# Linear memory's projection as seven block products in a one-core encoder layer

## The chip, the cores and the metric

The kernel runs on one core of one Trainium2 chip. The metric is the device time of one execution in microseconds (us), as the median of several executions. Of one execution there is also a trace from the hardware profiler: every instruction on each engine with its start and length. The engines are called as in the profile: PE is TensorE's matmul and PEld its weight load, DVE is VectorE, ACT is ScalarE, POOL is GpSimd, SP is SyncE, which here only issues DMAs.

## The reference

One inference step of one encoder layer, on 576 tokens (512 of a new stream, called the prompt, and 64 that continue a running stream) of width D = 1024, all in float32:

```
h = LN1(alpha*x + 0.5*FFN1(x))
z = h @ w_in      # q, k, v, o, i, f of the linear memory | q, k, v of attention | gates g_m, g_a
m = mLSTM(h)      # 4 heads of 256: head outputs normalised, times a gain and sigmoid(o)
y_ml  = m @ w_ml_proj                       # 1024 x 1024: the product that is changed
y_att = att @ w_att_proj
merged = sigmoid(g_m) * y_ml + sigmoid(g_a) * y_att
h = LN2(alpha*h + merged @ w_out)
y = LN3(alpha*h + 0.5*FFN2(h))
```

The outputs are y for both streams and the new states of convolution, linear memory and attention.

## The kernel before

Activations lie transposed: eight tiles of 128 features by 576 tokens. Each float32 product is made of three matmuls of rounded parts. A tile is split into **hi** (ScalarE rounds it) and **lo** (the remainder, by VectorE: tile minus hi), for weights and activations, and `mm3` adds hi·hi, hi·lo and lo·hi in PSUM. So every operand costs ScalarE and VectorE one pass each before TensorE can use it, and a weight tile of 128 x 1024 as much as an activation tile.

**Weights.** `plan` (from L430) lists all weight tiles in the order of use. `pump` (L248) loads the next raw tile on SP's queue into one of two `wr` buffers, and splits it into one of four pairs `wh`, `wl`; `take` and `done` (to L317) count them in and out. For the keys of the set ADDED the remainder is made by a transfer instead (`add_lo`, L195): ScalarE writes -hi, and a DMA on GpSimd's queue adds the raw weight from HBM to it.

**Order of the work.** TensorE's program is written in the order in which the Python code emits it; `later(dt, f)` on the object `od` puts f into a heap by due time, counted in TensorE's work, so that short pieces (transposes, norms) stand between the long products. On the other engines a scheduler orders the instructions by priority (`high_priority`, `issue_after`), and each engine works its list strictly in order.

**Stages.** FFN1 and LN1 (`Norm`, L536; `ffn`, L1158), the products with w_in with attention between them, attention's projection (`ap_pair`, L1808), the linear memory's four heads (L1841 to L2143), its projection (L2144 to L2193, 1041.7 to 1092.4 us), the output projection with LN2 (L2196 to L2205), FFN2 and LN3.

**Seven block products.** `seven` (L838) serves the FFNs and attention's projection. A pair of output column tiles j, j+1 (columns 1 and 2) by the two halves of the tokens is a 2 x 2 block product over two halves of the input tiles. In Winograd's form it needs seven products instead of eight, of sums of the weight blocks (`split_ds`, L209: a is the first column's weight as it is, u two sums, t two more, b half the second's) and of sums of the activation blocks (b11, b21, b22 as they are; t1 to t4 sums). Each product is four input tiles by three matmuls, on 288 columns, into one of three PSUM tiles X, Y, Z, in the order a·b11, a·b21, t·t2, u·t1, u·t3, t·b22, b·t4. After product n `step(n)` takes out what is complete.

**The projection.** Head 3 ends with the transposes of its normalised output `hf` and the last gate's product (`gate(7)`, 48 matmuls). `ht_split` splits the eight tiles of m (`HF`, called og in the profile) into hi and lo (`H`). Then eight plain products, one per column tile j, each 48 matmuls: for both halves of the tokens (256 and 320 columns) eight input tiles by three matmuls. `mp_cb` multiplies the result by the gate `sg` (called s in the profile) on VectorE, adds attention's half `matt` on GpSimd, which SP has loaded from HBM (`MD`) for all eight tiles, and splits the sum into `mg`, the output projection's input.

**The residual of LN2.** LN1's output stays in SBUF as hi and lo (it is the input of all products with w_in). LN2 makes alpha·h from it by two VectorE instructions per tile and half (`residual`, L562). LN2's own output is also written to HBM (`XD`, L1156), from where LN3 fetches it as one tile and needs one instruction.

## Time and profile before

| | |
|---|---|
| Executions before | 1549.29, 1549.52, 1552.53 us; median 1549.52 |
| Span of the profiled execution | 1546.8 us (its own time is not listed apart; median less span is 2.7) |
| PE busy | 1531.3 us, 11587 matmuls |
| DVE, ACT, POOL busy | 1160.4, 882.5, 196.6 us |
| Projection | 1041.7 to 1092.4 us, 384 matmuls |

The page gives first the span and the busy time of each engine, then the span in 40 slices with the granted TensorE clock, the DMA queues, the chain of work that ended last, and the costliest groups of instructions. A line of a group or of the timeline names the source line, the engine, the operation, what it writes and reads by the program's names (`wl<-wr,wh`: a weight's remainder from raw and hi), the shape, and in square brackets how long the engine had been idle before it and what ended that. Matmuls are pipelined, so two may overlap in a line of the timeline; the spacing of their starts is their price.

### The profile page before, as it was taken

What the parts mean: (1) busy time and instruction counts of PE and PEld (TensorE: products, weight loads), DVE (VectorE), ACT (ScalarE), POOL (GpSimd) and SP (SyncE); (2) the same over time, 40 slices, a digit from 0 to 9 for tenths busy, and PEclk for the clock granted to TensorE, in tenths of its full rate; (3) what the DMA queues carried; (4) which work ended last, traced back from release to release, by engine and by line L of the source; (5) the groups of instructions that cost most, each with busy time, mean ns of one, the idle gap of its engine ahead of it and who ended that gap; (6) DMA issues with size and microseconds to landing.
All of it is one profiled execution on the core that took longest, in us unless ns stands there. A gap on an engine that the chain in (4) does not pass through costs nothing.

```text
span 1546.8 us, 29458 instructions
## 1 busy us (share of the span) xinstructions
PE 1531.3 (99%) x11587; PEld 1516.3 (98%) x11587; DVE 1160.4 (75%) x2186; ACT 882.5 (57%) x1670; POOL 196.6 (13%) x370
## 2 busy tenths in 40 slices
PE   9999999999999999999999999999999999999997
PEld 9999999999999999999999999999999999999997
DVE  7877778756899767887677577775688787787756
ACT  7545446533766557777864877753456454557323
POOL 1000000100200015545200321102120000001000
PEclk9999999999999999999999999999999999999999
DMA  8322223535544449687544965542653223217244
GB/s 246 109 101 91 93 99 102 130 108 146 172 152 143 156 167 239 153 209 169 139 107 147 283 148 133 130 132 82 199 126 104 108 82 110 82 69 190 78 128 150
DMA packets 82228, 213.18 MB, mean 138 GB/s; under 512 B 9513, under 2 KB 23209, under 8 KB 82089
## 3 DMA queue, kind: packets, MB, share of 16 engines
q1 hardware_dynamic: 66088, 172.29, 33.8%
q0 software_dynamic: 14848, 37.30, 13.7%
q8 instruction: 91, 1.49, 0.4%
q10 hardware_dynamic: 1152, 1.70, 0.3%
q14 instruction: 49, 0.39, 0.1%
HBM read 174.82 MB, written 22.22 MB: 127 GB/s over the span
## 4 chain that ended last, share of the span: by engine, by line
PE 84%; DVE 7%; ACT 3%; DMA 3%; issue 2%; POOL 1%; SPq 0%; ACTq 0%; DVEq 0%; POOLq 0%
PE mm L133 69%; PE aux L133 14%; PE aux L143 2%; DVE wl L150 1%; DVE sc L1537 1%; DVE s L150 1%; DVE s L153 1%; ACT wh L147 1%; ACT sc L147 1%; DMA s<-in_xT 1%; DVE o L150 1%; DVE kl L150 1%; DVE sc L157 1%; DMA wr<-in_w_ap 0%; DMA kh<-kh 0%
## 5 line engine op out<-in xcount | busy, mean ns | idle before, releaser
L133 PE MATMUL mm<-s,wh 128*128 128x288 f32 (+2 forms) x3430 | 700.8, 298 | 0.7 <-DVE s L150 0.2
L133 PEld LDWEIGHTS mm<-s,wh 128*128 128x128 f32 x3430 | 548.3, 189 | 3.8 <-DVE s L150 1.6
L133 PE MATMUL mm<-s,wl 128*128 128x288 f32 (+2 forms) x1705 | 503.3, 295 | 0.0
L133 PEld LDWEIGHTS mm<-s,wl 128*128 128x128 f32 x1705 | 321.1, 188 | 0.2 <-DVE wl L150 0.2
L147 ACT ACTIVATE wh<-wr 128x1024 fp32r<-128x1024 f32 (+2 forms) x136 | 133.0, 979 | 141.0 <-PE mm L133 81.7
L133 PE MATMUL mm<-tx,wh 128*128 128x288 f32 x778 | 158.4, 296 | 0.0
L150 DVE TENSOR_TENSOR wl<-wr,wh 128x1024 fp32r<-128x1024 f32 (+2 forms) x97 | 108.9, 1126 | 57.1 <-ACT wh L147 57.0
L133 PEld LDWEIGHTS mm<-tx,wh 128*128 128x128 f32 x778 | 124.9, 188 | 0.0
L133 PE MATMUL mm<-tx,wl 128*128 128x288 f32 x383 | 113.0, 295 | 0.6 <-DVE wl L150 0.6
L925 ACT ACTIVATE wh<-wt 128x1024 fp32r<-128x1024 f32 x53 | 56.2, 1060 | 88.4 <-DVE wt L150 88.4
L150 DVE TENSOR_TENSOR wl<-wt,wh 128x1024 fp32r<-128x1024 f32 x53 | 64.7, 1222 | 52.3 <-ACT wh L925 51.0
L133 PE MATMUL mm<-h,wh 128*128 128x256 f32 (+2 forms) x384 | 78.3, 295 | 0.0
L150 DVE TENSOR_TENSOR wl<-wu,wh 128x1024 fp32r<-128x1024 f32 x50 | 61.2, 1224 | 21.6 <-ACT wh L925 21.6
L197 POOL DMA_DIRECT2D s<-s x16 | 13.7, 854 | 495.0 <-ACT s L147 252.8
L133 PEld LDWEIGHTS mm<-tx,wl 128*128 128x128 f32 x383 | 72.0, 188 | 0.9 <-DVE wl L150 0.9
L147 ACT ACTIVATE h<-h 128x288 f32<-128x288 f32 x80 | 34.9, 437 | 65.2 <-DVE h L150 65.1
L925 ACT ACTIVATE wh<-wu 128x1024 fp32r<-128x1024 f32 x50 | 52.9, 1058 | 32.7 <-PE mm L133 32.5
L150 DVE TENSOR_TENSOR wl<-ws,wh 128x1024 fp32r<-128x1024 f32 x53 | 64.6, 1219 | 0.1
L150 DVE TENSOR_TENSOR ws<-wu 128x1024 f32<-128x1024 f32 x53 | 64.5, 1217 | 0.0
L133 PEld LDWEIGHTS mm<-h,wh 128*128 128x128 f32 x384 | 61.5, 188 | 0.2
L925 ACT ACTIVATE ah<-wu 128x512 fp32r<-128x512 f32 x53 | 33.4, 631 | 44.8 <-PE mm L133 41.3
L133 PE MATMUL mm<-h,wl 128*128 128x256 f32 (+2 forms) x192 | 56.5, 294 | 0.0
(399 smaller groups left out, 3612.6 us busy)
## 6 DMA issues: line engine op xcount, KB each, us to landing
wu<-in_w_gu SPq DMA_DIRECT2D x80, 512.0 KB, 4.3
wr<-in_w_in SPq DMA_DIRECT2D x46, 512.0 KB, 3.7
wr<-in_w_dn SPq DMA_DIRECT2D x40, 512.0 KB, 3.6
wl<-in_w_in POOLq DMA_DIRECT2D x38, 512.0 KB, 6.8
wu<-in_w_in SPq DMA_DIRECT2D x26, 512.0 KB, 4.5
wr<-in_w_dn SPq DMA_DIRECT2D x20, 384.0 KB, 3.7
s<-s POOLq DMA_DIRECT2D x16, 288.0 KB, 3.7
wr<-in_w_ap SPq DMA_DIRECT2D x8, 512.0 KB, 3.6
```

Source lines behind the costliest of these rows:

```text
L133: PE.matmul(out, lhsT, rhs, start=start, stop=stop, **kw)
L143: PE.transpose(out, in_, idn)
L147: return ACT.activation(out, in_, func, **kw)
L150: return (eng or DVE).tensor_tensor(out, a, b, op=op)
L153: return DVE.scalar_tensor_tensor(out=out, in0=a, scalar=s, in1=b, op0=op0, op1=op1)
L157: return (eng or DVE).tensor_scalar(out=out, in0=a, scalar1=s1, scalar2=s2, op0=op0, **kw)
L197: return POOL.dma_start(lo, src, accum_op=ALU.add)
L925: self.last = ACT.activation(hi, src, AF.Copy)
L1537: DVE.tensor_tensor_reduce(out=out, in0=ps, in1=g, op0=ALU.add, op1=ALU.min, scale=-1.0, scalar=3e38, accum_out=acc)
```

## The change

The linear memory's projection takes the form of attention's projection: the plan lists four weights a, u, t, b per pair of column tiles, and `mp_pair` calls `seven`. The rows of w_ml_proj are regrouped on the host, even tiles first, so that the two halves of the input tiles are the first and the second tile of each head. `blocks(i)` makes head i's activation factors: it rounds and subtracts the plain tiles, and makes the four sums of half tiles on VectorE, in place in the two tiles of m; then it splits the sums. The remainder of the sums of heads 0 and 1, and of one of head 2's two, is made by `add_lo`, the rest on VectorE. Heads 0 and 1 are emitted while head 3 is still at work (`first_blocks`), heads 2 and 3 behind it. The remainders of a and b weights are made by `add_lo` too; u and t have their sums and remainders on VectorE, with buffers of their own (`q`). Attention's half is no longer loaded: for three pairs a DMA on GpSimd's queue adds it from HBM into the gated tile, and for the last pair it is loaded into two tiles and added on VectorE.

LN1 now writes its normed output to HBM (`XH`, 16 DMAs on SP's queue), and LN2 fetches it from there (8 DMAs on SP's queue) and needs one residual instruction per tile and half. The arguments `down` and `store` of `Norm` carry what `away` alone said before. Some buffers of the heads move to pools that end earlier (`mq`) to make the room.

In the instruction lists the matmuls of the projection are 336 instead of 384; TensorE's order ahead of the projection is the same.

The diff, cut to its core:

```diff
         def put(a, t):
             n = t.shape[1]
             ds["hi"] = act(hi[:, a:a + n], t)
+            if plan[c][0][0] == "dsmp" and what in "ab":
+                add_lo(lo[:, :n], hi[:, :n], plan[c][1])
+                return
             tt(lo[:, a:a + n], t, f(hi[:, a:a + n]), ALU.subtract)
 
         if what == "a":
             put(0, r1)
         elif what == "u":
-            own = plan[c][0][0] == "dsap" and plan[c][0][1] > 0
-            room = lambda: (slot(F32, opool[0], "o") if own else slot(F32))[:, :512]
+            mp_ = plan[c][0][0] == "dsmp"
+            own = mp_ or plan[c][0][0] == "dsap" and plan[c][0][1] > 0
+            def room():
+                if mp_:
+                    return qpool[0].tile([P, 512], F32, tag="q", name=nm("q"), bufs=4)
+                return (slot(F32, opool[0], "o") if own else slot(F32))[:, :512]
+
             q = ds["q"] = [room() for _ in range(2)]
             ds["r"] = [room() for _ in range(2)] if own else [q[1]] * 2
             r2 = ds["u"]
             for i in range(2):
-                tt(q[i], (r1[:, 512:], r2[:, :512])[i], r2[:, 512:], ALU.add)
+                with tc.issue_after(wst["blocks"].ins) if plan[c][0][:2] == ("dsmp", 2) else nullcontext():
+                    tt(q[i], (r1[:, 512:], r2[:, :512])[i], r2[:, 512:], ALU.add)
             for i in range(2):
                 put(512 * i, q[i])
         elif what == "t":
...
-    plan += [(("mp", j), ins["w_mp"][j]) for j in range(KT)]
+    for j in range(0, KT, 2):
+        a, b = ins["w_mp"][j], ins["w_mp"][j + 1]
+        plan += [(("dsmp", j, x), w) for x, w in (("a", a), ("u", b), ("t", None), ("b", b[:, :512]))]
     plan += [(("o", j), ins["w_o"][j]) for j in range(KT)]
     plan_ffn(2)
...
     class Norm:
-        def __init__(self, xs, scale, eps, gi, final=None, keep=False, away=None):
-            self.away = away
+        def __init__(self, xs, scale, eps, gi, final=None, keep=False, away=None, down=False, store=None):
+            self.away, self.down, self.store = away, down, store
...
                     act(dh, dh, AF.Identity, bias=b_)
-                    if self.away is None:
-                        SP.dma_start(XD[j][:, t0:t0 + n], dh)
+                    SP.dma_start(self.store[j][:, t0:t0 + n], dh)
                     act(hs(hi, hf), dh)
                     tt(hs(lo, hf), dh, hs(f(hi), hf), ALU.subtract)
...
 
-        own = name == "dsap"
+        own = name in ("dsap", "dsmp")
         product(X, "a", 1, "b11", True, False)
...
 
-    XD = [away("xd") for _ in range(KT)]
+    XD, XH = [away("xd") for _ in range(KT)], [away("xh") for _ in range(KT)]
...
                 ln = Norm(xs, 2.0 * ALPHA, 4.0 * EPS, gi, final, keep=final is None,
-                          away=[ins["xT"][:, k] for k in range(KT)] if prev is None else XD)
+                          away=[ins["xT"][:, k] for k in range(KT)] if prev is None else XD, down=True, store=XH)
...
+            if h == 3 and b == 4:
+                later(0, first_blocks)
 
         for b in range(5):
 
...
+    HB = [{} for _ in range(4)]
+    A, B = slice(HT_, T), slice(0, HT_)
+
+    def blocks(i):
+
+        r2, r1 = HF[2 * i], HF[2 * i + 1]
+        pool = htp[i > 1]
+        h2, l2, h1, hp_, lp_, hm, lm = (slot(F32R, pool, "H") for _ in range(7))
+        act(h2, r2)
+        tt(l2, r2, f(h2), ALU.subtract)
+        act(h1[:, :HT_], r1[:, A])
+        tt(h1[:, HT_:], r1[:, A], f(h1)[:, :HT_], ALU.subtract)
+        tt(r1[:, A], r1[:, A], r1[:, B], ALU.subtract)
+        tt(r1[:, B], r2[:, B], r1[:, B], ALU.subtract)
+        stt(r2[:, B], r1[:, A], -1.0, r2[:, B], ALU.mult, ALU.subtract)
+        stt(r2[:, A], r2[:, B], -1.0, r2[:, A], ALU.mult, ALU.subtract)
+        for hi, lo, r in ((hp_, lp_, r2), (hm, lm, r1)):
+            wst["rounded"] = act(hi, r)
+            if i < 2 or i == 2 and r is r1:
+                add_lo(lo, hi, r)
+            else:
+                wst["blocks"] = tt(lo, r, f(hi), ALU.subtract)
+        HB[i].update(b11=(h1[:, :HT_], h1[:, HT_:]), b21=(h2[:, A], l2[:, A]), b22=(h2[:, B], l2[:, B]),
+                     t4=(hp_[:, A], lp_[:, A]), t2=(hp_[:, B], lp_[:, B]),
+                     t1=(hm[:, A], lm[:, A]), t3=(hm[:, B], lm[:, B]))
+
+    htp = []
+    hts = ExitStack()
+
+    def first_blocks():
+        bstack.close()
+        htp.append(hts.enter_context(tc.tile_pool(name="ht0", bufs=14, side="right", reuse_waits="tile")))
+        for i in range(2):
+            blocks(i)
+
     mg = Act()
     sg = {}
...
     SP.dma_start(outs["conv"], conv_st)
     mstack.close()
-    rstack = ExitStack()
-    mgp = rstack.enter_context(tc.tile_pool(name="mg", bufs=16, side="right", reuse_waits="tile"))
-    hts = ExitStack()
-    htp = hts.enter_context(tc.tile_pool(name="ht", bufs=16, side="right", reuse_waits="tile"))
-    gmp = hts.enter_context(tc.tile_pool(name="gm", bufs=4, reuse_waits="tile"))
-    HT = Act()
-
-    def ht_split():
-        for o in HF:
-            hi, lo = slot(F32R, htp, "H"), slot(F32R, htp, "H")
-            act(hi, o)
-            yield tt(lo, o, f(hi), ALU.subtract)
-            HT.p.append((hi, lo))
-        for c in raw:
-            yield act(sg[c], sg[c], AF.Sigmoid)
-            gated.append(c)
-        yield None
-
-    gated = [0, 1, 2, 3, 7]
-    raw = [c - 56 for cs in FILL for c in cs]
-    od.bg.append((1300, ht_split()))
-    matt = [slot(F32) if j < 4 else slot(F32, gmp, "gm") for j in range(KT)]
-    for m, d in zip(matt, MD):
-        SP.dma_start(m, d)
+    htp.append(hts.enter_context(tc.tile_pool(name="ht1", bufs=14, reuse_waits="tile")))
+    sgp = hts.enter_context(tc.tile_pool(name="sg0", bufs=4, reuse_waits="tile"))
+    for i in range(2, 4):
+        with tc.high_priority(offset=100 * i):
+            blocks(i)
+    matt = {j: slot(F32) for j in (KT - 2, KT - 1)}
+    for j, m in matt.items():
+        SP.dma_start(m, MD[j])
     for j in range(4):
         sg[j] = slot(F32, sgp, "sg")
         SP.dma_start(sg[j], GD[j])
+    for cs in FILL:
+        for c in cs:
+            with tc.issue_after(wst["rounded"].ins):
+                act(sg[c - 56], sg[c - 56], AF.Sigmoid)
     gate(7, None, "s", AF.Sigmoid)
-    od.force(lambda: len(HT.p) == KT)
-
-    def mp_cb(j):
-        def cb(hf, ps):
-            od.force(lambda: j in gated)
-            s, m = hs(sg[j], hf), hs(matt[j], hf)
-            tt(s, s, ps, ALU.mult)
-            tt(m, m, s, ALU.add, POOL)
-            if len(mg.p) <= j:
-                mg.p.append((slot(F32R, mgp, "mg"), slot(F32R, mgp, "mg")))
-            hi, lo = mg.p[j]
-            act(hs(hi, hf), m)
-            tt(hs(lo, hf), m, hs(f(hi), hf), ALU.subtract)
-        return cb
-
-    for j in range(KT):
-        gemm(one(("mp", j)), HT, [mp_cb(j)])
+
+    def mp_pair(j):
+        X, Y, Z = bank("mm")[:, :HT_], bank("aux")[:, :HT_], bank("mm")[:, :HT_]
+        g1, g2 = sg[j], sg[j + 1]
+        o1, o2 = slot(F32, hp, "og"), slot(F32, hp, "og")
+        last = j == KT - 2
+
+        def split(e, cc=slice(0, T)):
+            m, (hi, lo) = sg[j + e], mg.p[j + e]
+            act(hi[:, cc], m[:, cc])
+            tt(lo[:, cc], m[:, cc], f(hi)[:, cc], ALU.subtract)
+
+        def step(n):
+            if n in (1, 3, 4):
+                with tc.high_priority(offset=100):
+                    act(*{1: (o1[:, A], X), 3: (o1[:, B], X), 4: (o2[:, B], Z)}[n], scale=-1.0 if n == 4 else 1.0)
+                return
+            with tc.high_priority(offset=60):
+                if n == 7:
+                    stt(g2[:, A], X, -1.0, g2[:, A], ALU.mult, ALU.mult)
+                else:
+                    o, ps = {2: (o1[:, A], Y), 5: (o2[:, B], X), 6: (o1[:, B], Z)}[n]
+                    with tc.issue_after(wst["blocks"].ins) if j + n == 2 else nullcontext():
+                        tt(o, o, ps, ALU.subtract if n == 5 else ALU.add)
+                if n == 5:
+                    tt(g2[:, B], g2[:, B], o2[:, B], ALU.mult)
+                if n == 6:
+                    tt(g1, g1, o1, ALU.mult)
+            if last:
+                e, cc = {5: (1, B), 6: (0, slice(0, T)), 7: (1, A)}.get(n, (0, None))
+                if cc is not None:
+                    with tc.high_priority(offset=60 if n == 7 else 0):
+                        tt(sg[j + e][:, cc], sg[j + e][:, cc], matt[j + e][:, cc], ALU.add)
+                        split(e, cc)
+            elif n > 5:
+                POOL.dma_start(sg[j + n - 6], MD[j + n - 6], accum_op=ALU.add)
+                split(n - 6)
+
+        mg.p += [(slot(F32R), slot(F32R)) for _ in range(2)]
+        seven("dsmp", j, HB, X, Y, Z, step)
+
+    for j in range(0, KT, 2):
+        mp_pair(j)
     hts.close()
     hstack.close()
     gate_close = gstack.close
 
-    ln2 = Norm(H, ALPHA, EPS, 1, keep=True)
+    ln2 = Norm(H, ALPHA, EPS, 1, keep=True, away=XH, store=XD)
+    with tc.issue_after(wst["load"].ins):
+        for j in range(KT):
+            ln2.fetch(j, SP)
     estack = ExitStack()
     epool = estack.enter_context(tc.tile_pool(name="early", bufs=1, reuse_waits="tile"))
     for i, key in enumerate(EARLY):
@@ -2201,7 +2268,6 @@
     for j in range(5):
         gemm(one(("o", j)), mg, [ln2.cb(j)])
     gemm([[(("o", j), KT)] for j in (5, 6, 7)], mg, [ln2.cb(j) for j in (5, 6, 7)], SKEW3, ["mm", "mm", "aux"])
-    rstack.close()
     gate_close()
     ln3 = ffn(ln2.out, 2, 2, ln2.d, outs["y"], ln2)
     ln3.close()
...
         "w_in": wtiles(np.concatenate([w_in[:, :4096], w_in[:, 4104:]], axis=1)),
         "w_if": w_if.reshape(P, KT * 64),
-        "w_mp": wtiles(a["w_ml_proj"][0]),
+        "w_mp": wtiles(a["w_ml_proj"][0].reshape(4, 2, P, D).swapaxes(0, 1).reshape(D, D)),
         "w_ap": wtiles(a["w_att_proj"][0]),
         "w_o": wtiles(a["w_out"][0]),
```

More of the change, by code (lines that the diff above doesn't have):

```diff
@@ L594, in collect @@
                     self.moments(j, hf, dh)
-                if j < KT - 1 and (self.away is None or j + 1 not in DS):
+                if j < KT - 1 and not (self.down and j + 1 in DS):
                     self.residual(j + 1, hf)
@@ L630, in shift @@
             self.shifted.add(hf)
-            if self.away is not None and hf == 1:
+            if self.down and hf == 1:
                 for j in range(2, LAST[1]):
@@ L673, in stats @@
             later(L_MEAN, lambda: self.centre(hf, bc, power))
-            later(J_SPREAD if hf and self.away is not None else L_SPREAD, lambda: self.spread(hf, dg))
+            later(J_SPREAD if hf and self.down else L_SPREAD, lambda: self.spread(hf, dg))
         def rsqrt(self, hf, st):
@@ L1953, in ml_kq @@
         ml_decay(h, st)
[L1954 removed]
+        qtail = mq.tile([P, 2, NS], F32, tag="qtail", name=nm("qtail"))
         for e in range(2):
```

30 lines of the change are left out of this document (16 added, 14 removed).

## The prediction

> **What bounds the kernel now.** I read the head of the profile's page first, for the span and the engine that fills it.
>
> ```profile
> span 1546.8 us, 29458 instructions
> PE 1531.3 (99%) x11587; PEld 1516.3 (98%) x11587; DVE 1160.4 (75%) x2186; ACT 882.5 (57%) x1670; POOL 196.6 (13%) x370
> PEclk9999999999999999999999999999999999999999
> PE 84%; DVE 7%; ACT 3%; DMA 3%; issue 2%; POOL 1%; SPq 0%; ACTq 0%; DVEq 0%; POOLq 0%
> ```
>
> TensorE is busy 99% of the span at the full granted clock, so a matmul taken away is time taken away, unless a wait takes its place. Then the stages around the projection, in the table of windows (columns: stretch, length, PE, PEld, DVE, ACT, POOL busy, granted clock, DMA share, GB/s), TensorE's first and last instruction of the projection (all matmuls that read a tile named H there), and TensorE's waits.
>
> ```profile
> 1030.00:1042.00 12.00, 12.00 (x93) 11.99 (x92) 9.10 (x20) 6.80 (x13) 1.20 (x1) 1.00 0.82 285
> 1042.00:1093.00 51.00, 51.00 (x389) 51.00 (x388) 26.44 (x42) 16.40 (x26) 12.03 (x15) 1.00 0.26 83
> 1093.00:1146.00 53.00, 53.00 (x403) 52.75 (x402) 41.38 (x96) 28.02 (x48) 8.51 (x10) 1.00 0.67 178
> ```
>
> ```profile
> L133 PE MATMUL mm<-H,wh x256: 279/296/310, 1041.7 to 1092.2; 128*128 128x256 f32 x64, 128*128 128x320 f32 x64
> L133 PE MATMUL mm<-H,wl x128: 281/294/308, 1042.0 to 1092.4; 128*128 128x256 f32 x64, 128*128 128x320 f32 x64
> ```
>
> ```profile
> PE aux L143 <- DVE ptl L150: 2.1, 4, 1.0
> ...
> PE aux L504 <- POOL one L487: 1.1, 1, 1.1
> ...
> PE mm L133 <- DVE wl L150: 0.6, 1, 0.6
> ```
>
> The projection takes 50.7 us (1041.7 to 1092.4) for 384 matmuls, 0.132 us each, with no wait inside: VectorE is busy about half of that time and ScalarE a third. In the whole run TensorE never waits longer than 1.1 us at once. But in the 12 us ahead of the projection VectorE is busy 9.1 us and ScalarE 6.8 us, so little room is left there, and that is where the change puts the new sums.
>
> **The gain.** Seven block products instead of eight: per pair of column tiles 7 products of 12 matmuls, 288 columns each; 4 pairs make 336 matmuls, 48 fewer. What a product of that shape takes stands where the attention's projection already works so: its first two products begin at
>
> ```profile
> 803.55 0.43 PE L133 MATMUL mm<-os,wh 128*128 128x288 f32 x2
> ...
> 805.13 0.42 PE L133 MATMUL aux<-os,wh 128*128 128x288 f32 x2
> ```
>
> 1.58 us apart, 0.132 per matmul, the same as before's mean. **Gain: 48 x 0.132 = -6.3 us.** I keep no bounds on it; count and rate are both seen.
>
> **Pair 0: the operands come late.** Before the first product, VectorE and ScalarE must make from four pairs of head outputs (blocks 0 to 3) the seven left factors each. The rows that price it, ScalarE and then VectorE, from the timeline (start, length, engine, line, out<-in, count):
>
> ```profile
> 1034.30 1.06 ACT L147 ACTIVATE wh<-wr 128x1024 fp32r<-128x1024 f32 x1 [2.99 <-PE mm L133]
> 1038.70 2.97 ACT L147 ACTIVATE H<-og 128x576 fp32r<-128x576 f32 x5
> 1041.94 0.44 ACT L147 ACTIVATE s<-mm 128x320 f32<-128x320 f32 x1 [0.27 <-PE mm L133]
> ...
> 811.56 1.16 ACT L147 ACTIVATE wh<-o 128x512 fp32r<-128x512 f32 x2 [1.00 <-PE mm L133]
> 810.15 0.41 ACT L147 ACTIVATE o<-mm 128x288 f32<-128x288 f32 x1 [1.23 <-PE mm L133]
> ```
>
> ```profile
> 1031.77 0.17 DVE L150 TENSOR_TENSOR mrs<-mrs,dn 128x5 f32<-128x5 f32 x1 [1.31 <-POOL mrs L533]
> 1031.97 1.69 DVE L157 TENSOR_SCALAR hf<-hf,mv,mrs 128x256 f32<-128x256 f32 x5
> 1034.89 1.79 DVE L153 SCALAR_TENSOR_TENSOR og<-aux,cols,og 128x512 f32<-128x512 f32 x4 [1.22 <-PE aux L143]
> 1037.26 1.22 DVE L150 TENSOR_TENSOR wl<-wr,wh 128x1024 fp32r<-128x1024 f32 x1
> 1039.41 4.33 DVE L150 TENSOR_TENSOR H<-og,H 128x576 fp32r<-128x576 f32 x6 [0.26 <-ACT H L147]
> ...
> 790.99 0.83 DVE L150 TENSOR_TENSOR o<-o 128x288 f32<-128x288 f32 x2
> 791.73 1.30 DVE L150 TENSOR_TENSOR wl<-s,wh 128x512 fp32r<-128x512 f32 x2
> ```
>
> Back to back the instructions overlap by about 0.1 us, so the chains are added with ScalarE 0.58 per 576 columns, 0.53 per 512, 0.31 to 0.32 per 288 or 320, and VectorE 0.67 per 576, 0.60 per 512, 0.37 per 288. TensorE's side:
>
> ```profile
> 1034.25 1.25 PE L143 MATMUL aux<-ident,hf 128*128 128x128 f32 x10
> ...
> 1041.60 0.31 PE L133 MATMUL mm<-s,wl 128*128 128x320 f32 x1
> 1041.74 0.40 PE L133 MATMUL mm<-H,wh 128*128 128x256 f32 x2
> ```
>
> Head 3's normalised output is done at 1033.6 (1031.97 + 1.69); I let it come at 1034.0, since ScalarE copies weights and block operands ahead of the last of its five parts. From there VectorE has no gap, in the changed program's order: block 1's remainder and four sums (0.67 + 5 x 0.37 = 2.5), four gate products of head 3 (1.6 of the 1.79 above), block 2's first remainder 0.67, two weight remainders of 512 (1.2), block 2's small remainder and four sums (5 x 0.37 = 1.85): 7.8 us, so block 2's sums are ready at **1041.8**. ScalarE then still has ahead of the first product's last operand, in its order: three roundings or negations of block 2 (one of hp, two of hm, 3 x 0.58), a b weight of 512 and its negation (2 x 0.53), block 3's 576 (0.58), a gate eviction (0.32) and block 3's 288 (0.31): 4.0 us, 1045.9 with hand-overs 1046.0; its remainder on VectorE 0.37 more and a hand-over, **1046.5**. TensorE, which still begins at 1041.7, does the products of blocks 0 to 2 (9 x 0.132) by 1042.9 and then waits. **+3.6 us.** Least: block 2's sums come 1.9 us sooner, because VectorE does block 1's in the gaps that it has before 1034.0 (1.31 us in the first row of its fence): 1.7. Most: block 3's remainder of 576 also stands ahead on VectorE (0.67) and eight hand-overs cost 0.2 more each: 5.9.
>
> The third product needs block 3's hp. ScalarE does it behind the split of pair 1's first weight (1.06, and only after the second product has released its buffer, about 1048.4): 1050.0, its remainder at 1050.8, while TensorE comes there at 1049.7 (1046.9 + 1.58 + 9 x 0.132). **+1.2 us** (0 to 2.4: a copy that finds its buffer free, or one more 1.06 ahead).
>
> **Pairs 1 to 3: weights by transfer.** The remainder of a and b weights now comes from an accumulating DMA on GpSimd's queue: ScalarE writes the negated hi, GpSimd issues, and the transfer adds the raw weight. These are the rows that price it; the fourth and fifth answer to the same line in the stretch 985 to 1020 and in the whole run.
>
> ```profile
> 996.21 1.07 ACT L147 ACTIVATE wl<-wh 128x1024 fp32r<-128x1024 f32 x1
> 997.58 0.93 POOL L197 DMA_DIRECT2D wl<-in_w_in  x1 [0.49 <-ACT wl L147]
> wl<-in_w_in POOLq DMA_DIRECT2D x38, 512.0 KB, 6.8
> DMA to landing us min/median/max: 5.3/5.3/5.4
> DMA to landing us min/median/max: 3.4/5.8/11.0
> s<-s POOLq DMA_DIRECT2D x16, 288.0 KB, 3.7
> wr<-in_w_mp SPq DMA_DIRECT2D x8, 512.0 KB, 3.4
> ```
>
> From the release of the buffers to a usable lo it is 1.0 + 1.0 on ScalarE, 0.5 to issue, then the landing: 7.8 us with 5.3, against about 9.5 us that TensorE works on the five products between. Pair 1 has some 1 us to spare. Pair 2's first weight stands on ScalarE behind the split of pair 0's gated tile, which itself waits for the attention half's accumulate (sixth row, 3.7 us): TensorE waits about **+1.3 us** there; pair 3 about 0. With a landing of 6.8, pairs 2 and 3 lose 1.5 us more each; with 11.0, 5.7 each; at 3.4 nothing is lost. I take 5.3, the landing of the transfers nearest in time (997 and 1008). That they share with the weight loads of the same moment speaks against it: the Trainium skill, page "DMA: Bandwidth & Descriptors", section "Issuing engines are not separate DMA queues", says that transfers of all issuing engines interleave on the same 16 DMA engines. By it the gate and attention tiles and the next weights that SP sends at the stage's start hold the accumulates back, and the longer landing, 1552.2 + 3.0, would be the time; the range 3.4 to 11.0 of one line's landings agrees that other traffic counts.
>
> **The change into the output projection.** The last pair ends with sums and splits on VectorE, where a weight remainder of 1024 (1.1) stands ahead of step 6, and another ahead of the remainder of the seventh tile; the eighth tile's first half can only follow the seventh product. The o stage starts at once with
>
> ```profile
> 1093.22 0.40 PE L133 MATMUL mm<-mg,wh 128*128 128x256 f32 x2
> ...
> 1093.58 0.40 PE L133 MATMUL mm<-mg,wh 128*128 128x256 f32 x2
> ```
>
> three matmuls in 0.36 us per input tile, so it asks for the seventh tile 6 x 0.36 = 2.2 us after the last product. After that product come step 7, two adds, two remainders and the weight's 1.1: the seventh tile is there at 3.3 (hi) to 4.7 (lo). **+2.4 us**; 0.9 if the weight's 1.1 falls elsewhere, 3.5 if both do not.
>
> **The parked normed input.** FFN1's norm writes 16 halves to HBM on SP's queue and the o stage fetches 8 tiles; in return 16 residual instructions of VectorE go, and that engine is at 41 of 53 us there (third window above), so nothing is gained. The weight loads of the in stage stand on SP behind those stores, which wait for ScalarE, and they already wait at that place:
>
> ```profile
> 383.91 8.39 SPq L266 DMA_DIRECT2D wr<-in_w_in  x3
> ...
> 390.00:400.00 10.00, 9.93 (x74) 9.72 (x73) 8.22 (x19) 7.05 (x17) 2.42 (x7) 1.00 0.54 175
> ```
>
> TensorE loses 0.1 there and waited 0.6 for a weight's remainder nearby (waits above). **+0.5 us**, 0 to 1.5 (a late load of three delays one split of 1.06 + 0.4).
>
> **Sum:** -6.3 + 3.6 + 1.2 + 1.3 + 2.4 + 0.5 = +2.7; span 1546.8 + 2.7 = 1549.5. Around the span lie 2.7 us (median 1549.52 - 1546.8; the executions ran from 1549.29 to 1552.53), so the time is **1552.2 us**. 0.2% of the time before, 3.1 us, is about what a measurement of this kernel can tell from no change: 1546.4 to 1552.6 is the same.
>
> **Rivals.** (1) **Faster:** every wait at its small end (1.7, 0, 0, 0.9, 0): -3.7, **1545.8**. For it speaks that TensorE nowhere waits more than 1.1 us now, so buffers run well ahead; against it, that ScalarE's order in front of the first product is fixed, 4.0 us of it after block 2's sums. (2) **Slower, by the landings:** from a landing of about 5.5 us on, pairs 2 and 3 wait for their weights; at the median 6.8 it is 3.0 more, **1555.2**. For it: 38 such transfers with that median. Against it: 5.3 for the nearest ones. (3) **Slower, by the clock:** the wait of 3.6 us is longer than any in the trace, where the clock is 1.00 in every window, so no row shows what TensorE does after it. If its clock fell by half behind the wait, two products would take 3.2 each instead of 1.6: **1555.4**. The Trainium skill, page "TensorE: Matmul & The Clock Gate", section "🔬 Part 1: The HAM clock gate (the "warmup" mystery)", says that the clock halves after an idle window of some 3.4 us and returns after as long a busy one; no run here shows it. (4) **Slower, by SP's queue:** the stores hold all three loads of the in stage, 1.5 more: **1553.7**. That the change doesn't do what it says I exclude: the order of the changed program has 48 matmuls fewer.
>
> **How the numbers follow.** Forecast 0.52, of which 0.30 the same, 0.20 slower (it lies 0.4 under the bound) and 0.02 faster; rival 1 0.16, faster; rival 2 0.18, slower; rival 3 0.07, slower; rival 4 0.07, 0.05 slower and 0.02 the same. Faster 0.18, same 0.32, slower 0.50. The range runs from rival 1, 1545.8, to rivals 2 and 4 together, 1556.7; all ends of the unknown costs together (5.9, 2.4, 4.3, 3.5, 1.5) would be 1560.8, which I leave out. The forecast's own range is 1550 to 1554.5.
>
> **What would show it.** TensorE's matmul count 11539. A wait of 3.6 us before the fourth block of the first product, put down to ScalarE or VectorE writing H; a second of about 1.2 in the third product; one of about 1.3 at pair 2's start for a DMA of wl from the projection's weights; 2.4 early in the o stage for the split of the last tiles. The stage from first product to first o matmul 50.5 us (44.4 + 6.1) instead of 50.7. The forecast is wrong if the first wait is under 2 or over 5, if a landing is over 5.5 us in this stage, or if the granted clock leaves 1.00.

## The result, and the profile after

The changed kernel takes **1570.96 us** (median of 4 executions, 1566.91 to 1571.21) against 1549.4 us for the kernel before (4 executions, 1548.99 to 1552.53): 1.27% slower by the ratio of the executions, 1.0127 with a 95% interval of 1.0112 to 1.0142 (the two medians alone stand at 1.0139). The forecast was 1552.2, its range ended at 1556.7.

The head of the profile's page of the changed kernel, as shown of the kernel before: span, busy time, granted clock by slice, chain by engine.

```profile
span 1569.5 us, 29513 instructions
...
PE 1535.8 (98%) x11539; PEld 1517.9 (97%) x11539; DVE 1174.8 (75%) x2217; ACT 905.5 (58%) x1712; POOL 201.2 (13%) x373
...
PEclk9999999999999999999999999998999999999999
...
PE 77%; DVE 9%; DMA 5%; issue 4%; ACT 3%; POOL 1%; DVEq 0%; SPq 0%; ACTq 0%; POOLq 0%
```

The 48 matmuls are gone (11587 to 11539), and yet PE is busy 4.5 us longer: matmuls went slower somewhere. One slice of the clock's row has an 8. TensorE's share of the chain fell from 84% to 77%. What TensorE waited for, in the whole run:

```profile
PE mm L133 <- ACT og L147: 10.9, 4, 5.4
PE mm L133 <- ACT H L147: 4.2, 2, 3.9
...
PE mm L133 <- DVE s L150: 1.5, 3, 1.1
...
PE aux L133 <- DVE qk L153: 0.8, 1, 0.8
PE mm L133 <- ACT s L147: 0.8, 1, 0.8
...
PE mm L133 <- DVE H L150: 0.4, 1, 0.4
```

The second and last rows are the forecast's waits of pair 0 (3.9 and 0.8 us). The first row, 10.9 us for `og` on ScalarE, is in none of its terms. The tile view of H (first fence) gives the start of the projection's first and last matmuls, and the output projection begins with the row of the second fence:

```profile
L133 PE MATMUL mm<-H,wh x192: 289/295/608, 1043.7 to 1111.1; 128*128 128x288 f32 x192
```

```profile
1111.36 0.40 PE L133 MATMUL mm<-s,wh 128*128 128x256 f32 x2
```

So the projection now takes 67.6 us (1043.7 to 1111.36), not 50.8. Its longest matmuls took 608 ns where the median is 295. By stages the 22.7 us that the span grew are:

| Stage | us | of which |
|---|---|---|
| ahead of the projection | +2.0 | 0.9 at 405 to 409, 0.85 at 1014, the rest spread |
| projection | +16.8 | -6.3 matmuls; +15.5 waits (10.9 + 4.2 + 0.4); +7.7 left over (6.2 half clock, 1.5 the rest) |
| behind it | +3.9 | 1.85 waits, the rest mostly the clock |

The 7.7 is 67.6 - 336 x 0.132 - 15.5, and most of it is the clock. Aligned stretches of the table of windows (columns as in the prediction: length, PE, PEld, DVE, ACT, POOL, clock, DMA share, GB/s):

```profile
1045.51:1048.93 3.42, 0.00 (x0) 0.00 (x0) 1.42 (x2) 3.37 (x7) 1.55 (x2) 1.00 0.61 184
1048.93:1052.34 3.41, 3.40 (x13) 3.19 (x14) 2.29 (x6) 0.41 (x1) 0.18 (x1) 0.50 0.95 159
...
1069.41:1072.82 3.41, 0.00 (x0) 0.00 (x0) 0.22 (x1) 0.94 (x2) 0.00 (x0) 1.00 0.94 173
1072.82:1076.23 3.41, 2.37 (x10) 2.37 (x11) 3.30 (x6) 2.81 (x5) 0.85 (x1) 0.50 0.09 17
1076.23:1079.65 3.42, 3.42 (x16) 3.42 (x16) 1.92 (x4) 1.15 (x2) 0.00 (x0) 0.50 0.94 149
...
1086.47:1089.89 3.42, 1.37 (x11) 1.13 (x9) 2.36 (x4) 1.85 (x4) 0.00 (x0) 1.00 1.04 179
1089.89:1093.30 3.41, 3.28 (x13) 3.28 (x14) 1.59 (x3) 1.19 (x4) 0.85 (x1) 0.50 0.56 76
1103.54:1106.95 3.41, 1.86 (x12) 1.62 (x12) 0.76 (x1) 0.46 (x2) 0.00 (x0) 1.00 0.82 225
1106.95:1110.37 3.42, 2.30 (x17) 2.30 (x18) 2.58 (x4) 2.46 (x4) 0.00 (x0) 1.00 0.00 1
```

After a stretch of 3.41 us without a matmul the next 3.41 us run at 0.50: 13 matmuls where 26 would fit. Behind the longest wait, which reaches into the next stretch, two stretches run at 0.50. The stretch with 1.37 us of work is followed by half clock too, the one with 1.86 is not. In the four halved stretches TensorE is busy 3.40, 2.37, 3.42 and 3.28 us; half of that, 6.2 us, is what the clock took. The other 1.5 are not the clock. A wait is counted from the end of a matmul (0.295 us), where without a wait the next would have started after 0.132: over seven waits that makes an estimate of 1.1.

The large wait is read on ScalarE. Its timeline where pair 0 passes to pair 1, and TensorE's row that waits:

```profile
1063.75 0.41 ACT L147 ACTIVATE og<-mm 128x288 f32<-128x288 f32 x1 [0.42 <-PE mm L133]
1064.06 0.62 ACT L147 ACTIVATE wh<-q 128x512 fp32r<-128x512 f32 x1
1071.88 0.68 ACT L147 ACTIVATE s<-sg 128x576 fp32r<-128x576 f32 x1 [7.20 <-DMA sg<-md]
1072.47 1.04 ACT L147 ACTIVATE wh<-wr 128x1024 fp32r<-128x1024 f32 x1
1073.42 0.39 ACT L147 ACTIVATE og<-mm 128x288 f32<-128x288 f32 x1
```

```profile
1073.86 0.85 PE L133 MATMUL mm<-H,wh 128*128 128x288 f32 x2 [5.37 <-ACT og L147]
```

ScalarE stands idle for 7.2 us because the next instruction in its order, the split of pair 0's gated tile, waits for the transfer that adds attention's half. Behind it stands an eviction of 0.39 us, step 3 of pair 1 (step 1 was the first row). TensorE has done four products of pair 1, and the fifth adds into the bank that this step must empty first. The three later waits for `og`, in pairs 2 and 3, follow the same pattern: ScalarE idles 2.42, 2.34 and 3.04 us for such an addition, with evictions behind it. In 1062.6 to 1064.9 five transfers were issued (group, KB each, median us to landing):

```profile
wr<-in_w_mp SPq DMA_DIRECT2D x2, 512.0 KB, 5.7
sg<-md POOLq DMA_DIRECT2D x2, 288.0 KB, 9.2
wl<-in_w_mp POOLq DMA_DIRECT2D x1, 256.0 KB, 9.1
```

The additions took 9.2 us, where a 288 KB addition took 3.7 in the kernel before.

At the output projection's start the two waits of the forecast are there (first two rows), the 4 us behind them have a mean clock of 0.59 (third row), and a weight's remainder stands on VectorE ahead of the split that is waited for (last two):

```profile
1114.45 0.38 PE L133 MATMUL mm<-s,wh 128*128 128x256 f32 x1 [0.78 <-ACT s L147]
1115.90 0.39 PE L133 MATMUL mm<-s,wh 128*128 128x256 f32 x1 [1.07 <-DVE s L150]
```

```profile
1116.50:1120.50 4.00, 4.00 (x20) 4.00 (x19) 0.91 (x2) 0.42 (x1) 0.00 (x0) 0.59 0.97 310
```

```profile
1113.96 1.22 DVE L150 TENSOR_TENSOR wl<-wr,wh 128x1024 fp32r<-128x1024 f32 x1
1115.10 0.75 DVE L150 TENSOR_TENSOR s<-s,s 128x576 fp32r<-128x576 f32 x1
```

### The profile page after: what moved, and what is told of

It reads as the page before. It is cut to its first block, busy times and chain, and to the rows that moved or that the text cites. A ratio compares the mean times of both kernels' runs of the same rounds, so it can differ in the third digit from the quotient of the medians.

```text
span 1569.5 us, 29513 instructions
## 1 busy us (share of the span) xinstructions
PE 1535.8 (98%) x11539; PEld 1517.9 (97%) x11539; DVE 1174.8 (75%) x2217; ACT 905.5 (58%) x1712; POOL 201.2 (13%) x373
## 4 chain that ended last, share of the span: by engine, by line
PE 77%; DVE 9%; DMA 5%; issue 4%; ACT 3%; POOL 1%; DVEq 0%; SPq 0%; ACTq 0%; POOLq 0%
PE mm L133 62%; PE aux L133 14%; DVE wl L150 2%; PE aux L143 1%; DMA wr<-in_w_dn 1%; DVE s L150 1%; DMA kh<-kh 1%; DVE s L153 1%; ACT wh L147 1%; DVE sc L1548 1%; ACT sc L147 1%; DVE o L150 1%; DMA wl<-in_w_in 1%; DVE kl L150 1%; DMA s<-in_xT 0%
## 5 line engine op out<-in xcount | busy, mean ns | idle before, releaser
L133 PE MATMUL mm<-s,wh 128*128 128x288 f32 (+2 forms) x3654 | 747.7, 298 | 2.7 <-DVE s L150 1.3
L133 PEld LDWEIGHTS mm<-s,wh 128*128 128x128 f32 x3654 | 585.6, 189 | 6.4 <-DVE s L150 3.0
L133 PE MATMUL mm<-s,wl 128*128 128x288 f32 (+2 forms) x1817 | 537.1, 296 | 0.1
L133 PEld LDWEIGHTS mm<-s,wl 128*128 128x128 f32 x1817 | 343.0, 189 | 0.4 <-DMA wl<-in_w_in 0.3
L150 DVE TENSOR_TENSOR wl<-wr,wh 128x1024 fp32r<-128x1024 f32 (+2 forms) x89 | 96.2, 1084 | 57.1 <-ACT wh L147 57.1
L147 ACT ACTIVATE s<-s 128x576 fp32r<-128x576 f32 (+6 forms) x94 | 50.0, 558 | 20.5 <-DVE s L150 7.9
```

What stands on the lines that cost most here:

```text
L133: PE.matmul(out, lhsT, rhs, start=start, stop=stop, **kw)
L147: return ACT.activation(out, in_, func, **kw)
L150: return (eng or DVE).tensor_tensor(out, a, b, op=op)
```

## The experiments

Times are medians, with the ratio to the kernel before on the same chip and its 95% interval. All are versions of the changed kernel unless said otherwise.

### 1. The split emitted later

```diff
-                split(n - 6)
+                pend.append(lambda e=n - 6: split(e))
 # in step(4) of the next pair, behind its eviction:
+                while n == 4 and pend:
+                    pend.pop(0)()
```

> Only the place of the splits of the gated tiles changes: for pairs 0 to 2 they stand behind the fourth step of the next pair, so behind its three evictions on ScalarE; the transfers that add attention's half stay as they are. Theory 1 (ScalarE works in order, and the split that waits for the transfer, 8.5 us after its issue at 1063.4, holds the eviction that the third product of the next pair needs): the waits of TensorE for og on ScalarE, 10.9 us in four places, go down to under 2, and the half clock behind them (about 4.6 us lost) goes too; time 1570.8 - 9 - 4.6 = about 1557, 1554 to 1560. Theory 2 (the remainders of the a and b weights come late because they are made by transfers): TensorE waits as long as before, now for weights; 1568 or more. Theory 3 (the 20 us are spread over many things): about 1565.

Measured: 1570.65 us, 1.0139 (1.0124 to 1.0154). No theory was tested, for the order on ScalarE did not move: the split still stands ahead of the eviction.

```profile
1071.15 0.68 ACT L147 ACTIVATE s<-sg 128x576 fp32r<-128x576 f32 x1 [7.17 <-DMA sg<-md]
1071.74 1.04 ACT L147 ACTIVATE wh<-wr 128x1024 fp32r<-128x1024 f32 x1
1072.68 0.39 ACT L147 ACTIVATE og<-mm 128x288 f32<-128x288 f32 x1
```

Here the place in the source did not decide the place on the engine; the scheduler put it back.

### 2. Weight remainders on VectorE

```diff
-            if plan[c][0][0] == "dsmp" and what in "ab":
-                add_lo(lo[:, :n], hi[:, :n], plan[c][1])
-                return
```

> Only the remainders of the a and b weights of the projection are made by VectorE instead of by accumulating transfers. Theory 2 (these transfers bind): the waits of 5.4, 2.2, 1.2 and 2.2 us go, 1556 to 1560. Theory 1 (the attention half's transfers bind, through ScalarE's queue): with three transfers fewer per pair on the same queue the attention half lands sooner (5 to 6 us instead of 8.5), so only some 3 to 5 us of the 20 go, 1565 to 1568, and TensorE still waits for og on ScalarE.

Measured: 1570.0 us, 1.0135 (1.0119 to 1.0152). TensorE still waits 9.1 us for og on ScalarE, in three places, the longest 4.9 now in pair 2. The second theory, which is the forecast's own rival with the landings of the weights, falls; the gain of 3 to 5 us that the first expected did not come either, although the additions of attention's half landed sooner, in 5.5 us in the median instead of 6.9. (The trace is of the fastest execution, 1566.40 us.)

### 3. The parked normed input alone

The kernel before, with the stores of FFN1's norm and the fetches by LN2, and nothing else.

> The kernel before with one part of the change: the first norm writes its output to HBM, and the second norm fetches its residual from there. The trace of the changed kernel is 0.9 to 1.2 us late between 405 and 641, ahead of all other parts. Theory: these stores cost that, +1.0 us (1550.4), as two small delays near 405 and 409, and nothing later. Rival: the lateness comes from something else that moved, and this is 0; or the fetches in the output projection disturb it, +2 or more.

Measured: 1550.09 us, 1.0010 (1.0000 to 1.0019). The order of the matmuls is that of before, and between 309 and 409 they fall 1.0 us behind it. One of the two places is

```profile
405.19 0.51 PE L133 MATMUL aux<-dg,one 128*128 128x320 f32 x1 [0.35 <-DVE dg L157]
```

where the kernel before has no wait. The cost is of the size expected, at the edge of what the timing resolves.

### 4. Products in the waits

```diff
+            idle = name == "dsmp" and {(0, "a", 1): (3, 29), (2, "t", 0): (0, 41), (4, "t", 0): (0, 16)}.get((j, what, half))
             for i in range(4):
+                if idle and i == idle[0]:
+                    for _ in range(idle[1]):
+                        PE.matmul(Z, parts[ids["a"] if j == 0 else ids["t"]][0][:, :P], blocks[0]["b21"][0], ...)
```

> The changed kernel with extra products at three places where TensorE waits: 29 matmuls before the fourth block of the first product, 41 before the third product of pair 1, 16 before that of pair 2, on operands that are there, into a PSUM tile that the next product overwrites. They are extra work, 29 x 0.132 = 3.8, 5.4 and 2.1 us, and fill the waits of 3.9, 5.4 and 2.2. Theory (the clock is halved because TensorE stood idle): the granted clock stays 1.00 over the stage, the waits' places keep their length, and the time is shorter by the 6.2 us lost at half clock, about 1564.5, although 86 matmuls are added. Rival (the halving has another cause, power for one): the clock still falls to 0.50 and the time is 1571 or more.

Measured: 1576.09 us, 1.0174 (1.0157 to 1.0191), 5 us longer than without the extra products: the waits did not stay where they were. The clock kept 1.00 through pair 0, but pair 1 then waited 4.0 us for a weight by transfer, pair 2 still waited 3.3, and the clock fell behind each. The extra products of pairs 1 and 2 were also put in the wrong place: ahead of the third product, as the expectations of all runs up to here name it, while the wait is ahead of the fifth (step 3's eviction, above). So this run could not price the clock. Experiment 7 repeats it at one place.

### 5. The splits held, attention's half loaded, plain parts first

Three mendings of the two causes seen, and the first and third also together. Held: the split of experiment 1, with an order that the scheduler keeps.

```diff
+                while n == 4 and pend:
+                    with tc.issue_after(ev.ins):     # ev: the eviction of step 4
+                        pend.pop(0)()
```

> As the first experiment, but the splits of the gated tiles are held behind the fourth step's eviction by an order that the scheduler keeps; in the first one its instruction order on ScalarE stayed as it was (the split of the first gated tile ahead of the next pair's second eviction), so it told nothing. Theory 1 (the split that waits for attention's half blocks the evictions behind it in ScalarE's order): the waits for og on ScalarE in the projection, 10.9 us in four places, fall below 2; with the half clock behind them 8.9 + 4.6 us go: 1557, 1555 to 1561. What may be late next is the first weight of pairs 2 and 3 by transfer, up to 2 us each. Theory 2 (late weights bind): TensorE waits as long, put down to a DMA of wl; 1567 or more.

Measured: 1566.59 us, 1.0110 (1.0095 to 1.0125). The waits for og on ScalarE are gone. But the time fell by 4, not by 13: 5.2 us came back as waits for og on VectorE. Its timeline shows the same pattern: a sum of raw weights waits 5.74 us for its load, and step 5 stands behind it.

```profile
PE mm L133 <- DVE og L150: 5.2, 2, 3.0
PE mm L133 <- ACT H L147: 3.9, 1, 3.9
PE mm L133 <- DMA wl<-in_w_mp: 1.9, 1, 1.9
```

```profile
1072.99 0.69 DVE L150 TENSOR_TENSOR q<-wr,wr 128x512 f32<-128x512 f32 x1 [5.74 <-DMA wr<-in_w_mp]
...
1075.60 0.45 DVE L150 TENSOR_TENSOR og<-og,mm 128x288 f32<-128x288 f32 x1
```

Loaded: the addition by transfer undone for all pairs.

```diff
+        if not last:
+            for e in range(2):
+                matt[j + e] = slot(F32, hp, "og")
+                SP.dma_start(matt[j + e], MD[j + e])
...
-                POOL.dma_start(sg[j + n - 6], MD[j + n - 6], accum_op=ALU.add)
+                tt(sg[j + n - 6], sg[j + n - 6], matt[j + n - 6], ALU.add)
                 split(n - 6)
```

> Attention's half is loaded ahead, two tiles per pair on SP's queue at the pair's start, and added on VectorE for every pair (the changed kernel does so for the last one); the splits stay where they are. It undoes the transfer part of the change. Theory 1: the gated tile is complete 1 us after step 6, the split has nothing to wait for, and the waits for og fall below 2 us: 1557, 1554 to 1561; six more sums of 0.7 us on VectorE cost nothing. Theory 2: no gain over 2 us, 1568 or more.

Measured: 1559.97 us, 1.0068 (1.0053 to 1.0083), 11 us less than the changed kernel by the medians (9 by the ratios), of the 13 expected. Here the split stays in its place and has nothing to wait for:

```profile
PE mm L133 <- ACT H L147: 3.9, 1, 3.9
PE mm L133 <- DVE og L150: 1.7, 1, 1.7
PE mm L133 <- DMA wl<-in_w_mp: 1.3, 1, 1.3
```

```profile
1071.46 0.69 DVE L150 TENSOR_TENSOR q<-wr,wr 128x512 f32<-128x512 f32 x1 [3.82 <-DMA wr<-in_w_mp]
```

The 10.9 us for og on ScalarE are gone; 1.7 remains on VectorE, where a sum waits for its raw weight (last row). The first theory holds. The plain loads were not quick either: two of them, issued beside the same three weight transfers, took 7.2 us. But a load can be issued before its tile is needed, while the addition can only be issued when the gated tile is complete.

Plain parts first: for heads 2 and 3 the roundings that products 1 and 2 read, ahead of the sums.

```diff
+    for i in range(2, 4):
+        with tc.high_priority(offset=500):
+            blocks(i, 0)          # h2, l2, h1
     for i in range(2, 4):
         with tc.high_priority(offset=100 * i):
-            blocks(i)
+            blocks(i, 1)          # the four sums and their splits
```

> For heads 2 and 3 the plain parts (hi and lo of the tiles as they are, which the first two products read) are emitted ahead of the sums (which the third and fourth read). Theory (the wait of 3.9 us in the first product is the order of ScalarE and VectorE in front of it, block 3's plain tile behind block 2's sums): that wait falls below 0.7, the third product's stay about 0.4 each, the half clock after the first wait (1.7 us) goes, and the negated weight for pair 1 moves back behind two evictions, so pair 1's start waits up to 2.5 us: 1566 to 1568, 3 to 5 less than the changed kernel. Rival: the sums are late instead, the wait moves to the third product with the same 3.9: 1570.

Measured: 1566.49 us, 1.0104 (1.0082 to 1.0126). The 3.9 us are gone; 2.0 of it comes back in the fourth product, where a remainder of head 2's second sum is made by transfer, and 2.0 at pair 1's start, as expected for its weight. The trace is of the fastest of four executions (1560.73 to 1567.96), and in it the waits for og on ScalarE are 4.7 us, not 10.9: it shows the moved waits, but not the median.

```profile
1052.33 0.40 PE L133 MATMUL mm<-H,wh 128*128 128x288 f32 x1 [2.03 <-DMA H<-og]
1060.31 0.40 PE L133 MATMUL mm<-H,wl 128*128 128x288 f32 x1 [2.01 <-DMA wl<-in_w_mp]
```

Held and plain parts first together:

> The held splits and the plain parts first, together. If the two causes are separate, their gains add: 1570.8 - 13.5 - 4 = about 1553, 1550 to 1557. If one only moves the other's wait, it is no better than the better of the two by more than 1 us. What is left over the kernel before would be the output projection's start (2.0 us of waits and its half clock 1.7), 0.9 from the first norm's stores and 0.8 in head 3, against the 6.3 us of matmuls saved.

Measured: 1560.95 us, 1.0084 (1.0065 to 1.0103). Against 1570.96 that is -10.0, where the two alone gave -4.4 and -4.5. By the ratios the gains are 2.6 and 3.6 alone and 6.7 together. So the gains add within the spread of these runs, as separate causes would give; the 1553 expected did not come, since the held split had brought 4 us and not 13. That the causes are wholly separate is not shown: in the trace of plain parts first the waits for og fell too.

### 6. All mended, step by step

Loaded, plain parts first, and two remainders taken back from transfers to VectorE:

```diff
-            if i < 2 or i == 2 and r is r1:
+            if i < 2:
...
-            if plan[c][0][0] == "dsmp" and what in "ab":
+            if plan[c][0][0] == "dsmp" and what == "b":
```

> Attention's half loaded ahead, plain parts first, and by VectorE instead of by transfer the remainder of head 2's second sum and those of the a weights. Theory (the loss is a set of waits in the orders of ScalarE and VectorE, each removable): in the projection 0.7 us of waits left in pair 0 and up to 1.7 behind a late raw weight on VectorE, stage 46 to 48 us instead of 67.6; ahead of it 2.0 us and at the output projection's start 3.5 us later than the kernel before as they are: about 1550, 1547 to 1553. Rival: more work on VectorE (a remainder of 1.1 us per pair, six sums of 0.7) makes it the bound and the waits move there: 1556 or more.

Measured: 1552.13 us, 1.0017 (1.0009 to 1.0026). That is inside the range expected, and the rival's 1556 did not come. The projection took 50.9 us in the trace, not 46 to 48: pair 0 waited 2.15 us for og on ScalarE, and 6.83 us from 1049.21 on ran at half clock. Then the first column of the output projection takes both halves of the tokens tile by tile:

```diff
-        gemm(one(("o", j)), mg, [ln2.cb(j)])
+        gemm(one(("o", j)), mg, [ln2.cb(j)], *([JOINT] if j == 0 else []))
```

> As the one before, and the output projection's first column takes both halves of the tokens tile by tile, so that it asks for the seventh tile after 4.8 us instead of 2.2. Theory (its start loses 1.9 us of waits for the last two gated tiles and 1.7 at half clock): both go, 3 us less than the version before it, about 1547, 1545 to 1550, at or under the kernel before. Rival: the second column then waits for the norm's shift instead, and it is the same within 1.

Measured: 1550.47 us, 1.0009 (1.0001 to 1.0017). The waits of 0.8 and 1.1 at the output projection's start are gone, 1.2 for the norm's shift comes back. The gain of 1.7 us lies between the theory (3) and the rival (under 1): both have a part. Of the projection:

```profile
PE mm L133 <- DVE H L150: 1.0, 1, 1.0
...
PE mm L133 <- ACT H L147: 0.4, 1, 0.4
```

```profile
1044.00:1092.00 48.00, 46.31 (x344) 45.40 (x343) 45.32 (x78) 32.00 (x56) 3.43 (x4) 1.00 0.55 153
```

The projection takes 47.25 us here (50.8 before), the clock is 1.00 throughout, and VectorE is busy 45.3 of 48 us. Last, pair 0's weight sums are held behind head 3's last query tile:

> As the version with the joint start of the output projection, and the four weight sums of pair 0 on VectorE are held behind head 3's last query tile. Theory (two of these sums stand between the steps of that tile's convolution, and TensorE waits 0.8 us for it at 1014): that wait goes and the time is 0.8 us less than 1550.5, so 1549 to 1550, no longer measurably above the kernel before. Rival: the sums then delay the decay products behind them, and the same 0.8 us are lost there.

Measured: 1549.1 us, 0.9999 (0.9990 to 1.0008). The wait of 0.8 at 1014 is gone, though 0.8 us is less than the two intervals can tell apart in the time. This version is as fast as the kernel before, not faster.

### 7. Products in one wait

The version with attention's half loaded (1559.97), with the 29 extra matmuls of experiment 4 in pair 0's wait alone.

> The version with attention's half loaded ahead (1560.0), with 29 extra matmuls (3.8 us) before the fourth block of the first product, in the wait of 3.9 us there; they write into a PSUM tile that the next products overwrite. In that version the clock was halved for 6.8 us from 1047.9 on, inside and behind this wait. Theory (idle time halves the clock): granted clock 1.00 through pair 0, the products of pair 0 at 1.6 us each from the start, and the time 2 to 3 us shorter with 29 matmuls more: 1557 to 1558, unless what follows waits for the same thing later. Rival (load or power halves it): the clock falls all the same, 1560 or more.

Measured: 1562.97 us, 1.0088 (1.0074 to 1.0103). The stretches of its pair 0 and of what follows:

```profile
1045.00:1048.60 3.60, 3.60 (x28) 3.37 (x26) 1.39 (x2) 3.60 (x8) 1.52 (x2) 1.00 0.91 222
1048.60:1060.00 11.40, 10.78 (x76) 10.10 (x76) 9.89 (x20) 8.19 (x14) 1.07 (x2) 1.00 0.52 111
1060.30:1063.70 3.40, 0.18 (x2) 0.00 (x0) 2.58 (x5) 1.08 (x2) 0.86 (x1) 1.00 1.07 235
1063.80:1067.00 3.20, 1.79 (x7) 1.79 (x8) 0.00 (x0) 0.00 (x0) 0.00 (x0) 0.50 1.04 339
```

With TensorE kept busy the clock stays at 1.00 where it was halved for 6.8 us in the version without the extra products; it falls only at 1063.7, behind a stretch of 3.4 us with 0.18 us of work. That idleness halves it is shown. The time is not better: TensorE came to pair 1 with its weight's transfer still under way and waited 4.7 us there, the other part of what was expected ("unless what follows waits").

## Why the prediction was wrong

- **The gain** held: 48 matmuls fewer, 6.3 us, and the mended projection shows the room (47.25 us).
- **Pair 0** held in size: 3.6 forecast and 3.86 measured, then 1.2 and 0.8. Its cause is shown by the plain parts put first. ScalarE's chain behind block 2's sums was 4.0 forecast and took 4.1 (1044.79 to 1048.88). Both sides of the difference came over 2 us later than forecast, TensorE at 1043.74 instead of 1041.7 and the last operand at 1048.9 instead of 1046.5; that they moved together is in part luck.
- **Pairs 1 to 3** is the step that failed. The forecast saw that the split of the gated tile waits for attention's half, and named only the weight behind it on ScalarE. Behind it stand also the next pair's evictions, and within a pair each eviction is due one product later (1.6 us). It put the landing of the half at 3.7, the median of 16 additions elsewhere in the kernel before; of five transfers issued together the medians here were 5.7 to 9.2. Together this made 10.9 us of waits instead of 1.3, all of them ahead of the fifth and sixth products of pairs 1 to 3 and none at a pair's start, where the forecast had them. The half's transfer undone took 11 us off the time.
- **The second rival** had late transfers as its reason, but those of the weights. In the changed kernel's projection TensorE never waits for one, and their removal alone changed nothing (1570.0). Late raw weights and remainders matter only once the first cause is gone (1.7 and 1.3 us).
- **The third rival, the clock,** was right, had a chance of 0.07, and its price of 3.2 us was for one wait: the stage lost 6.2 to it and the output projection's start about 1.7 more. The Trainium skill, page "TensorE: Matmul & The Clock Gate", section "🔬 Part 1: The HAM clock gate (the "warmup" mystery)", has the clock halve after an idle window of some 3.4 us and the window run freely. The halvings here begin at 1048.93, 1072.82, 1089.89 and 1117.19, which are multiples of 3.413 apart (7, 12 and 20), as a free-running window gives. But a window need not be all idle: with 2.05 us without a matmul it was enough, and with 1.74 (1113.78 to 1117.19, 1.67 us busy), with 1.55 not. No sharp bound comes out of the runs: in experiment 1 the stretch 1086.22 to 1089.63 was idle for 1.81 us, in experiment 3 that from 628.90 to 632.31 for only 1.12, and half clock followed the second and not the first.
- **The output projection's start:** 2.4 forecast, 1.85 measured, without the clock.
- **The parked input:** 0.5 forecast, 0.9 to 1.0 in the traces. **Missed** was 0.85 at 1014: weight sums of pair 0 stand on VectorE between the steps of head 3's convolution. Holding them removed it.

The sum of what was found, -6.3 + 3.9 + 0.8 + 10.9 + 6.2 + 1.5 + 1.9 + 0.9 + 0.85 + about 1.7 of clock at the output projection's start, is 22.35, against 22.7 measured; the 1.5 is a remainder of the stage and closes its sum by itself. Even all ends of the forecast's unknown costs together (1560.8) stayed 10 under the time, because the evictions and the repeated clock were in none of them. (These ends take the landing at 6.8, not at the 11.0 that the forecast names as possible. With 11.0 they would come to 1569.2, near the time by luck, since no wait here was for a weight. And rival 4 adds 1.5 us to a sum that already holds 0.5 of the same 1.5.) The range was set too narrow by a missing mechanism, not by a mis-sized term.

What stays open: why the landings grew to 9.2 us was not tried apart; that the five transfers share the DMA engines (as the Trainium skill's page "DMA: Bandwidth & Descriptors", section "Issuing engines are not separate DMA queues", has it) fits the rows, and was not shown. Two rows speak for it: plain loads of two such tiles in such a crowd took 7.2 us, and without the weights' transfers the additions took 5.5 in the median instead of 6.9. Why undoing the weights' transfers alone gained nothing is not settled either.

## What to carry to other kernels

Where an instruction waits for a transfer, list everything behind it on its engine up to the next thing TensorE needs, evictions first, and take the landing with all transfers of the same moment under way. In a form of product whose banks are reused within 1.6 us, no instruction on the evicting engines may wait long for a transfer. And price an idle gap of TensorE of about 2 us or more with the half clock behind it, each time that it occurs, as likely and not as sure: the gap of 2.19 us here was followed by it, that of 2.16, which fell into two windows (1.55 and 1.12), was not.

## What the runs showed of the hardware beyond that

The granted clock falls to 0.50 on a grid of 3.413 us, and the grid's phase differs from run to run. The same wait of 3.86 us in pair 0 was followed by 3.41 us at half clock in the changed kernel (halved from 1048.93, where the wait ends at 1048.94) and by 6.83 us with attention's half loaded (halved from 1047.92, with the wait until 1049.61). So a kernel with waits of 1 to 2 us can have a wider spread: the version with the joint start ran from 1546.74 us (mean granted clock 0.999) to 1554.53 (0.996), the kernel before on the same chip from 1547.56 to 1550.97. In the profile of the parked input alone the clock fell at 632.31 for 3.41 us behind waits that stand in the kernel before at the same place without it. That the phase makes the spread is argued from this, not tried.
